# Moving the transposes and output products of the stick-breaking heads to later steps of the projection that covers them

## The chip, the cores and the metric

The kernel runs on one core of one Trainium2 chip. The metric is the device time of one execution in microseconds (us), as the median of the runs shown. Engines are named as in the profile: PE (TensorE matmuls), PEld (its weight loads), DVE (VectorE), ACT (ScalarE), POOL (GpSimd), SP (the queue that issues most DMAs).

## The reference, cut to what matters

A trunk of two layers over 256 positions of width 2048, all in float32. The first layer mixes sparse attention (10 heads, "A") with dilated attention (6 heads, "B"); the second mixes stick-breaking attention (8 heads, "C") with forgetting attention (8 heads, "D"). Each layer is one norm, one wide input projection, the heads, a gate, one output projection and the residual sum. The part that the change touches most is the stick-breaking head:

```python
z = jnp.einsum('bqhd,bshd->bhqs', qb, k).astype(F32) * (HEAD_DIM ** -0.5)
before = (key_pos[None, :] < qpos[:, None])[None, None]
log_1m = jnp.where(before, jax.nn.log_sigmoid(-z), 0.0)
tail = lax.cumsum(log_1m, axis=3, reverse=True) - log_1m
w = jnp.where(before, jnp.exp(jax.nn.log_sigmoid(z) + tail), 0.0)
return jnp.einsum('bhqs,bshd->bqhd', w.astype(v.dtype), v)
...
return x + (y * jax.nn.silu(gate)) @ w_out
```

## The kernel before, in words

The weights (about 165 MB) stream in once, cut into jobs. A job is the projection of both 128-row halves of the activations with one block of weight columns, mostly 512 wide: q, k, v and gate of one head of B, C or D, or q and gate of two heads of A. The jobs of the second layer are C0, F1, G1, C2 to C7, D0 to D7; F1 (264 wide: q and k of head C1, and the forget columns) and G1 (256 wide: its v and gate) share the columns of one head. A job walks over 16 row tiles of 128. To keep float32 accuracy on matmuls of a rounded type, each weight tile is split into an upper part (`whi`, by ACT, line 269) and the rest (`wlo`, by DVE, line 270), and each row tile takes three products for each half of the rows (lines 305, 306, 308). Splits cover two row tiles at a time (a "half" in the code; here a pair), so a job has eight pairs, and `split` (line 342) is called so that the split of a pair stands in the program three pairs ahead of its products.

Nothing reorders the work: the order is the order in which the code is written (manual schedule). What is left of a head after its job's projection (evacuating PSUM, transposes, scores, softmax or stick-breaking sums, products with v) is a generator that is started when its job's products have all been issued. It is advanced from inside the next jobs' projections: `tick` (line 293) counts a step for each row tile of a 512-wide job (for about each second row tile in F1 and G1), and a generator that said `yield n` goes on after n steps. So a 512-wide job offers 16 steps, and each engine gets the head's instructions between those of the running projection, in its own queue.

A stick-breaking head, in that order: at once, `scaled_qk` and `vg1` take q, k, v and gate out of PSUM (ACT lines 737, 749, 402; DVE lines 738, 751, the reciprocal 752, two products 755 that write the gate tile `u`, and 405). Then `stick` yields, and on PE `turn` (line 364) transposes q and k (four) and the gate `u` (two); ACT and DVE split the result (373, 374, 375) and ACT copies the gate (422, `uT`). After two steps come the scores (PE 800 and 379 to 381, then DVE `z` 803, ACT 805 to 807, DVE 808, the cut 392 and 393 into `sph` and `spl`), after five more the sums `pW` (812 to 815, then 816, 817, 820), one step on `pl` (822), and some steps on `weigh_out`: the products with v (379 to 381 and 430), the product with the gate (435, `y`) and its cut into `yh` and `yl` (392, 393).

`heads_a` does two sparse heads per job in the same manner; its last yields are the ones ahead of `turned(1, ...)`, the transposes of the second head's weights, and ahead of the products with v (687 to 689).

Of the kernel before, what the change touches and what calls it, by code (L numbers as in the profile page):

```python
# [159 lines left out]
def trunk(ctx, tc, x, xT, g1, w0, wo0, w1, wo1, bf, gf, consts, rope, out):  # L160
# [186 lines left out]
    def rotate(dst, src, cos, sin, r, m):  # L347

        n = r * m
        t1 = hp.tile([P, 512], F32, name="rot1", tag="rt1")  # L350
        t2 = hp.tile([P, 512], F32, name="rot2", tag="rt2")
        pair = lambda a: a.rearrange("p (r m two) -> p r m two", r=r, two=2)
        wide = lambda a: a.rearrange("p (r m) -> p r m", r=r)
        cb = cos.unsqueeze(1).to_broadcast([P, r, m]) if r > 1 else wide(cos)
        sb = sin.rearrange("p (m two) -> p m two", two=2).unsqueeze(1)
        sb = sb.to_broadcast([P, r, m // 2, 2]) if r > 1 else pair(sin)
        nc.vector.tensor_tensor(wide(t1[:, 0:n]), wide(src), cb, op=OP.mult)
        nc.vector.tensor_tensor(pair(t2[:, 0:n]), pair(src)[:, :, :, ::-1], sb, op=OP.mult)  # L358
        nc.gpsimd.tensor_tensor(dst, t1[:, 0:n], t2[:, 0:n], op=OP.add)  # L359

    def turn(srcs):
        pt = pa.tile([P, 512], F32, name="tp", tag="tp", bufs=2)
        for i, s in enumerate(srcs):
            nc.tensor.transpose(pt[:, i * P:(i + 1) * P], s, ident)  # L364
        return pt
# [24 lines left out]
    def cut(dst, src):  # L390

        nc.scalar.activation(dst[0], src, AF.Copy)  # L392
        nc.vector.tensor_tensor(dst[1], src, dst[0].bitcast(F32), op=OP.subtract)
# [18 lines left out]
    def gates(u, sc):  # L412

        for th in range(NT):
            t = slice(th * P, (th + 1) * P)
            nc.vector.tensor_scalar(u[:, t], u[:, t], sc[:, th:th + 1], None, op0=OP.mult)
# [23 lines left out]
    def soft(qk, nb):  # L440

        q0, k0, q1h, q1l, kh, kl = qk
        pS = pa.tile([P, 384], F32, name="s", tag="s", bufs=1)
        nc.tensor.matmul(pS[:, 0:P], q0, k0, start=True, stop=True)  # L444
        three(pS[:, P:384], q1h, q1l, kh, kl)
        sn = hp.tile([P, 384], F32, name="sn", tag="sn", bufs=2)
        nm = hp.tile([P, NT], F32, name="nm", tag="nm", bufs=2)
        l = hp.tile([P, NT], F32, name="l", tag="l", bufs=2)
        for th, s in BLK:
            nc.vector.tensor_tensor_reduce(sn[:, s], pS[:, s], nb[:, s], op0=OP.add, op1=OP.min, scale=1.0,  # L450
                                           scalar=3.0e38, accum_out=nm[:, th:th + 1])
            nc.scalar.activation(sn[:, s], sn[:, s], AF.Exp, scale=-1.0, bias=nm[:, th:th + 1],  # L452
                                 accum_out=l[:, th:th + 1])
        return sn, l

    def factor(l, rs):
        sc = hp.tile([P, NT], F32, name="sc", tag="sc", bufs=2)
        nc.vector.reciprocal(sc, l)
        if rs is not None:
            nc.vector.tensor_tensor(sc, sc, rs, op=OP.mult)  # L460
        return sc
# [178 lines left out]
    def heads_a(ps, h):  # L640
        qk = hp.tile([P, 512], F32, name="qk", tag="qk")
        u = hp.tile([P, 2, NT, P], F32, name="u2", tag="u2", bufs=1)
        tgs = {}
        for th in range(NT):
            rotate(qk[:, th * 256:(th + 1) * 256], ps[th][:, 0:256], rt[:, th, 0:P], rt[:, th, 256:384], 2, P)
            tgs[1 - th] = hp.tile([P, 256], F32, name="tg", tag="tg")
            nc.scalar.activation(tgs[1 - th], ps[1 - th][:, 256:512], AF.Tanh, scale=hr0[:, 1 - th:2 - th])
        for th in (1, 0):
            nc.vector.scalar_tensor_tensor(u[:, :, th, :], tgs[th].rearrange("p (a b) -> p a b", a=2), 1.0,
                                           ps[th][:, 256:512].rearrange("p (a b) -> p a b", a=2),  # L650
                                           op0=OP.add, op1=OP.mult)
        yield 4
        pt = turn([qk[:, 0:P], qk[:, P:256], qk[:, 256:384], qk[:, 384:512]])
        f = hp.tile([P, 256], F32, name="qqf", tag="qkf", bufs=1)
        hi = hp.tile([P, 256], F32R, name="qqh", tag="qkh", bufs=1)
        lo = hp.tile([P, 256], F32R, name="qql", tag="qkl", bufs=1)
        nc.scalar.activation(hi, pt[:, 256:512], AF.Copy)
        nc.scalar.activation(f, pt[:, 0:256], AF.Copy)
        nc.vector.tensor_tensor(lo, pt[:, 256:512], hi.bitcast(F32), op=OP.subtract)
        yield 2  # L660
        js = [slice(j * P, (j + 1) * P) for j in range(2)]

        ph, pl = (hp.tile([P, 2, SEQ], F32R, name="pA" + n, tag="i" + n, bufs=1) for n in "hl")
        p1h, p1l = (hp.tile([P, 2 * P], F32R, name="pB" + n, tag="v") for n in "hl")

        def turned(j, pr):
            pt = turn([pr[:, 0:P], pr[:, P:SEQ], pr[:, SEQ:384]])
            cut((ph[:, j, :], pl[:, j, :]), pt[:, 0:SEQ])
            cut((p1h[:, js[j]], p1l[:, js[j]]), pt[:, SEQ:384])

        sm = []
        for j in range(2):
            sm.append(soft((f[:, js[j]], kA, hi[:, js[j]], lo[:, js[j]], kAh, kAl), nbA))
            yield 2
            gates(u[:, j].rearrange("p a b -> p (a b)"), factor(sm[j][1], hr0))
        yield 1
        turned(0, sm[0][0])
        yield 2
        turned(1, sm[1][0])
        pt = turn([u[:, j, th] for j in range(2) for th in range(NT)])  # L680
        uT = hp.tile([P, 512], F32, name="uTA", tag="rl")
        nc.scalar.activation(uT, pt, AF.Copy)
        yield 3
        po = pa.tile([P, 512], F32, name="o", tag="o", bufs=1)
        vh, vl = vAs
        flat = lambda t: t.rearrange("p a b -> p (a b)")
        three_of(po, vh[:, 0], vl[:, 0], flat(ph), flat(pl), True, False)
        o1 = po.rearrange("p (a b c) -> p a b c", a=2, b=2)[:, :, 1, :]
        three_of(o1, vh[:, 1], vl[:, 1], p1h, p1l, False, True)
        y = hp.tile([P, 512], F32, name="yA", tag="rl")  # L690
        nc.vector.tensor_tensor(y, po, uT, op=OP.mult)
        kt = YPOS[f"A{h}"]
        cut([flat(t[:, kt:kt + 2, :]) for t in ys], y)
# [102 lines left out]
    def stick_head(qk, v, uT, kt):  # L796

        k1, q1, k0h, k0l, qh, ql = qk
        pZ = pa.tile([P, 384], F32, name="s", tag="s", bufs=1)
        nc.tensor.matmul(pZ[:, 0:P], k1, q1, start=True, stop=True)  # L800
        three(pZ[:, P:384], k0h, k0l, qh, ql)
        z = hp.tile([P, 384], F32, name="z", tag="sn")
        nc.vector.tensor_tensor(z, pZ, smask, op=OP.add)
        sp = hp.tile([P, 384], F32, name="sp", tag="sp", bufs=1)
        nc.scalar.activation(sp, z, AF.Abs)
        nc.scalar.activation(sp, sp, AF.Exp, scale=-1.0)
        nc.scalar.activation(sp, sp, AF.Ln, bias=1.0)
        nc.vector.scalar_tensor_tensor(sp, z, 0.0, sp, op0=OP.max, op1=OP.add)
        cut((sph[:, P:512], spl[:, P:512]), sp)
        yield 5  # L810
        pW = pa.tile([P, 384], F32, name="s", tag="s", bufs=1)
        nc.tensor.matmul(pW, tris[0], sph[:, P:512], start=True, stop=False)
        nc.tensor.matmul(pW, tris[0], spl[:, P:512], start=False, stop=False)
        nc.tensor.matmul(pW[:, 0:256], tris[1], sph[:, 0:256], start=False, stop=False)
        nc.tensor.matmul(pW[:, 0:256], tris[1], spl[:, 0:256], start=False, stop=True)
        nc.vector.tensor_tensor(z, pW, z, op=OP.add)
        nc.scalar.activation(z, z, AF.Exp)
        ph = hp.tile([P, SEQ], F32R, name="ph", tag="ph", bufs=1)
        pl = hp.tile([P, SEQ], F32R, name="pl", tag="pl", bufs=1)
        nc.scalar.activation(ph, z[:, P:384], AF.Copy)  # L820
        yield 1
        nc.vector.tensor_tensor(pl, z[:, P:384], ph.bitcast(F32), op=OP.subtract)
        yield 2
        weigh_out(ph, pl, z[:, 0:P], v, uT, kt, True)

    def stick(qk, v, u, kt):
        yield 2
        t = qk_turned([qk[:, 384:512], qk[:, 256:384], qk[:, 0:P], qk[:, P:256]])
        uT = gate_turned(u, True)
        yield 2  # L830
        yield from stick_head(qk_of(t), v, uT, kt)
# [150 lines left out]
```

## Time and profile before

| | us |
|---|---|
| median of 3 runs | 937.32 (937.15 to 938.77) |
| profiled execution | 937.25 |
| its span, first to last instruction | 935.5 |
| PE busy | 916.2 |
| DVE busy | 618.4 |
| ACT busy | 488.4 |

The span is what lies between the first and the last instruction; 1.75 us of the profiled execution lie around it. Busy time of an engine is the time in which one of its instructions ran; the rest of the span it either waited for another engine or had nothing to do. PE's matmuls overlap by a little, so the start of one to the start of the next is the time that it costs, and the duration in a row is longer than that (a 512-wide product: starts 0.23 us apart, rows of 0.39). A row ends in brackets with the idle time of its engine just before it, and with the instruction that ended that wait.

### The profile page before, as it was taken

The numbers are of one execution on the slowest core, as the hardware profiler recorded it, in microseconds if no ns is written. First come the engines' busy times: TensorE is split into PE (matmuls) and PEld (weight loads), VectorE is DVE, ScalarE is ACT, GpSimd is POOL, SyncE is SP. The second block draws the span as 40 slices with busy tenths as digits, with TensorE's granted clock in tenths as the row PEclk, the third lists the DMA queues.
The fourth block names the chain that finished last, engine by engine and source line by source line (L and its number), as shares of the span: only waits on it lengthen the run. The fifth ranks groups of instructions, "written<-read, shape, count | busy, mean of one in ns | idle before, by whom it ended". The sixth has DMA issues, their size and how long they took to land.

```text
span 935.5 us, 12005 instructions
## 1 busy us (share of the span) xinstructions
PE 916.2 (98%) x4489; PEld 767.3 (82%) x4489; DVE 618.4 (66%) x1053; ACT 488.4 (52%) x859; POOL 48.5 (5%) x68
## 2 busy tenths in 40 slices
PE   9999999999999999999999999999999999999996
PEld 6988888888888888888798777777888888888886
DVE  7667877766666665555566666666767666666563
ACT  7645545555455555555465555555555555555450
POOL 0021100000000000000000000000000000000110
PEclk9999999999999999999999999999999999999999
DMA  9954454544544454455275444445655555555542
GB/s 360 355 190 168 149 180 166 192 141 178 180 141 147 163 185 176 180 186 187 88 231 191 168 180 150 141 159 180 227 174 169 177 181 186 180 180 180 180 180 91
DMA packets 27323, 168.78 MB, mean 180 GB/s; under 512 B 3168, under 2 KB 3712, under 8 KB 9344
## 3 DMA queue, kind: packets, MB, share of 16 engines
q1 hardware_dynamic: 25920, 164.70, 49.7%
q0 software_dynamic: 768, 2.12, 0.8%
q10 hardware_dynamic: 576, 1.19, 0.3%
q8 instruction: 35, 0.57, 0.2%
q14 instruction: 24, 0.20, 0.1%
HBM read 165.89 MB, written 2.11 MB: 180 GB/s over the span
## 4 chain that ended last, share of the span: by engine, by line
PE 92%; DVE 4%; ACT 2%; issue 2%; DMA 0%; POOL 0%; SPq 0%; POOLq 0%; DVEq 0%; ACTq 0%
PE pj L305 28%; PE pj L306 28%; PE pj L308 28%; PE tp L364 3%; DVE e L752 1%; DVE wlo L270 1%; PE s L380 1%; PE s L444 1%; PE o L430 1%; ACT whi L269 1%; DMA w0yh<-in_w_in_dram 0%; PE s L379 0%; PE o L380 0%; PE s L381 0%; ACT e L749 0%
## 5 line engine op out<-in xcount | busy, mean ns | idle before, releaser
L270 DVE TENSOR_TENSOR wlo<-raw,whi 128x1024 fp32r<-128x1024 f32 (+3 forms) x300 | 357.7, 1203 | 174.1 <-ACT whi L269 172.5
L305 PE MATMUL pj<-whi,xh 128*128 128x512 f32 (+3 forms) x992 | 383.9, 389 | 0.6 <-ACT whi L269 0.6
L306 PE MATMUL pj<-whi,xl 128*128 128x512 f32 (+3 forms) x992 | 376.8, 381 | 0.0
L269 ACT ACTIVATE whi<-raw 128x1024 fp32r<-128x1024 f32 (+3 forms) x300 | 301.4, 1024 | 77.7 <-PE pj L306 71.6
L308 PE MATMUL pj<-wlo,xh 128*128 128x512 f32 (+3 forms) x992 | 297.1, 381 | 0.1
L308 PEld LDWEIGHTS pj<-wlo,xh 128*128 128x128 f32 x992 | 183.5, 188 | 37.0 <-DVE wlo L270 0.5
L305 PEld LDWEIGHTS pj<-whi,xh 128*128 128x128 f32 x992 | 186.6, 188 | 32.8 <-ACT whi L269 1.8
L306 PEld LDWEIGHTS pj<-whi,xl 128*128 128x128 f32 x992 | 186.7, 188 | 31.3 <-DVE xl L518 0.2
L305 PE MATMUL pj<-whi,yh 128*128 128x512 f32 (+1 forms) x248 | 96.0, 387 | 0.0
L306 PE MATMUL pj<-whi,yl 128*128 128x512 f32 (+1 forms) x248 | 94.9, 383 | 0.0
L308 PE MATMUL pj<-wlo,yh 128*128 128x512 f32 (+1 forms) x248 | 76.7, 383 | 0.0
L308 PEld LDWEIGHTS pj<-wlo,yh 128*128 128x128 f32 x248 | 46.6, 188 | 9.2
L305 PEld LDWEIGHTS pj<-whi,yh 128*128 128x128 f32 x248 | 46.6, 188 | 8.7
L306 PEld LDWEIGHTS pj<-whi,yl 128*128 128x128 f32 x248 | 46.7, 188 | 8.6
L452 ACT ACTIVATE sn<-sn,nm 128x128 f32<-128x128 f32 (+1 forms) x48 | 21.5, 449 | 55.3 <-DVE nm L450 55.3
L392 ACT ACTIVATE yh<-y 128x256 fp32r<-128x256 f32 x22 | 9.2, 418 | 41.4 <-DVE y L437 24.0
L480 ACT ACTIVATE sq<-xs 128x512 f32<-128x512 f32 x23 | 14.3, 622 | 29.4 <-DVE xs L703 26.8
L752 DVE RECIPROCAL e<-e 128x256 f32<-128x256 f32 x16 | 28.1, 1753 | 0.5
L359 POOL TENSOR_TENSOR qk<-rot,rot 128x256 f32<-128x256 f32 x22 | 15.8, 738 | 238.3 <-DVE rot L358 238.3
L737 ACT ACTIVATE qk<-pj,rr 128x128 f32<-128x128 f32 x32 | 10.0, 364 | 29.3 <-PE pj L308 29.3
L364 PE MATMUL tp<-cons,u 128*128 128x128 f32 x64 | 12.0, 282 | 9.4 <-DVE u L755 9.1
L738 DVE TENSOR_SCALAR qk<-pj,rstd 128x128 f32<-128x128 f32 x32 | 9.8, 347 | 16.4 <-ACT qk L737 16.4
(226 smaller groups left out, 753.5 us busy)
## 6 DMA issues: line engine op xcount, KB each, us to landing
raw<-in_w_in_dram SPq DMA_DIRECT2D x108, 1024.0 KB, 4.8
raw<-in_w_out_dram SPq DMA_DIRECT2D x32, 1024.0 KB, 4.8
raw<-in_w_in_dram SPq DMA_DIRECT2D x4, 672.0 KB, 9.9
raw<-in_w_in_dram SPq DMA_DIRECT2D x4, 528.0 KB, 3.5
w0yl<-in_w_in_dram SPq DMA_DIRECT2D x4, 512.0 KB, 6.9
xs<-in_x_dram SPq DMA_DIRECT2D x4, 512.0 KB, 11.3
raw<-in_w_in_dram SPq DMA_DIRECT2D x4, 512.0 KB, 4.0
xst<-in_xT_dram SPq DMA_DIRECT2D x5, 256.0 KB, 6.2
```

Of the source, the lines that this page charges most:

```text
L269: nc.scalar.activation(hi, rw, AF.Copy)
L270: nc.vector.tensor_tensor(lo, rw, hi.bitcast(F32), op=OP.subtract)
L305: nc.tensor.matmul(o, a, wh, start=(kt == 0), stop=False)
L306: nc.tensor.matmul(o, b, wh, start=False, stop=False)
L308: nc.tensor.matmul(o, a, wl, start=False, stop=(kt == KT - 1))
L359: nc.gpsimd.tensor_tensor(dst, t1[:, 0:n], t2[:, 0:n], op=OP.add)
L364: nc.tensor.transpose(pt[:, i * P:(i + 1) * P], s, ident)
L452: nc.scalar.activation(sn[:, s], sn[:, s], AF.Exp, scale=-1.0, bias=nm[:, th:th + 1], accum_out=l[:, th:th + 1])
L480: nc.scalar.activation(j, xs[:, th, c * 512:(c + 1) * 512], AF.Square, accum_out=ss[:, i, th, c:c + 1])
L737: nc.scalar.activation(qk[:, th * 256:th * 256 + P], ps[th][:, 0:P], AF.Copy, scale=rr[:, sgn, th:th + 1])
L738: nc.vector.tensor_scalar(qk[:, th * 256 + P:(th + 1) * 256], ps[th][:, P:256], r1[:, th:th + 1], None, op0=OP.mult)
L752: nc.vector.reciprocal(e, e)
```

## The change

Three numbers, no other edit. A stick-breaking head turns q, k and gate four steps after its job's end instead of two (`stick`, line 827). The products with v stand three steps after the split of the weights `pl`, instead of two (`stick_head`, line 823). Of two sparse heads, the second's transposes, and the gate's that follow them, stand three steps after the first's instead of two (`heads_a`, line 678). All later parts of these heads move with them: the scores and sums of a stick-breaking head by two steps, its outputs by three, the outputs of two sparse heads by one. No instruction is added or taken away.

```diff
         turned(0, sm[0][0])
-        yield 2
+        yield 3
         turned(1, sm[1][0])
...
         nc.vector.tensor_tensor(pl, z[:, P:384], ph.bitcast(F32), op=OP.subtract)
-        yield 2
+        yield 3
         weigh_out(ph, pl, z[:, 0:P], v, uT, kt, True)
...
     def stick(qk, v, u, kt):
-        yield 2
+        yield 4
         t = qk_turned([qk[:, 384:512], qk[:, 256:384], qk[:, 0:P], qk[:, P:256]])
```

On PE in job F1, where head C0 is turned, the order before is, from the third row tile's last products on (`pj` are the two PSUM tiles of the job, `tp` is where the transposes go):

```order
L308 MATMUL pj_4215<-wlo,xh 128x264
L308 MATMUL pj_4216<-wlo,xh 128x264
L364 MATMUL tp<-cons,qk 128x128 x4
L364 MATMUL tp<-cons,u 128x128 x2
L305 MATMUL pj_4215<-whi,xh 128x264
L306 MATMUL pj_4215<-whi,xl 128x264
L305 MATMUL pj_4216<-whi,xh 128x264
L306 MATMUL pj_4216<-whi,xl 128x264
L308 MATMUL pj_4215<-wlo,xh 128x264
```

The turn stands after three of the 16 row tiles, in the middle of the second pair. Of the changed kernel, the same place of the turn, with the end of one row tile ahead of it:

```order
L305 MATMUL pj_4215<-whi,xh 128x264
L306 MATMUL pj_4215<-whi,xl 128x264
L305 MATMUL pj_4216<-whi,xh 128x264
L306 MATMUL pj_4216<-whi,xl 128x264
L308 MATMUL pj_4215<-wlo,xh 128x264
L308 MATMUL pj_4216<-wlo,xh 128x264
L364 MATMUL tp<-cons,qk 128x128 x4
L364 MATMUL tp<-cons,u 128x128 x2
L305 MATMUL pj_4215<-whi,xh 128x264
```

It now stands after seven row tiles, in the middle of the fourth pair, so that pair's `wlo` is wanted ahead of the turn.

On DVE at the same place, from the end of job C0 on (`pj_4035` and `pj_4036` are C0's PSUM tiles, the 528-wide `wlo` are F1's pairs), before:

```order
L738 TENSOR_SCALAR qk<-pj_4036,rstd 128x128
L751 TENSOR_SCALAR e<-e 128x256
L752 RECIPROCAL e<-e 128x256
L755 SCALAR_TENSOR_TENSOR u<-pj_4035,rstd,e 128x128
L755 SCALAR_TENSOR_TENSOR u<-pj_4036,rstd,e 128x128
L405 SCALAR_TENSOR_TENSOR v<-pj_4035,rstd,v 128x128
L270 TENSOR_TENSOR wlo<-raw,whi 128x528 x2
L375 TENSOR_TENSOR qkl<-tp,qkh 128x384
L270 TENSOR_TENSOR wlo<-raw,whi 128x528 x2
L803 TENSOR_TENSOR z<-s,cons 128x384
```

And in the changed kernel:

```order
L752 RECIPROCAL e<-e 128x256
L755 SCALAR_TENSOR_TENSOR u<-pj_4035,rstd,e 128x128
L755 SCALAR_TENSOR_TENSOR u<-pj_4036,rstd,e 128x128
L405 SCALAR_TENSOR_TENSOR v<-pj_4035,rstd,v 128x128
L270 TENSOR_TENSOR wlo<-raw,whi 128x528 x4
L375 TENSOR_TENSOR qkl<-tp,qkh 128x384
L270 TENSOR_TENSOR wlo<-raw,whi 128x528
L270 TENSOR_TENSOR wlo<-raw,whi 128x512
L803 TENSOR_TENSOR z<-s,cons 128x384
```

Up to the first `wlo` nothing moved; two more `wlo` stand ahead of `qkl`.

On DVE at the end of job C2 (`y` and `yl` are the outputs of head C1, `pj_4576` and `pj_4577` the PSUM tiles of C2), before:

```order
L822 TENSOR_TENSOR pl<-z,ph 128x256
L270 TENSOR_TENSOR wlo<-raw,whi 128x1024
L435 TENSOR_TENSOR y<-o,uT 128x128 x2
L393 TENSOR_TENSOR yl<-y,yh 128x256
L270 TENSOR_TENSOR wlo<-raw,whi 128x1024 x2
L738 TENSOR_SCALAR qk<-pj_4576,rstd 128x128
L738 TENSOR_SCALAR qk<-pj_4577,rstd 128x128
```

And in the changed kernel:

```order
L822 TENSOR_TENSOR pl<-z,ph 128x256
L270 TENSOR_TENSOR wlo<-raw,whi 128x1024 x2
L435 TENSOR_TENSOR y<-o,uT 128x128 x2
L393 TENSOR_TENSOR yl<-y,yh 128x256
L738 TENSOR_SCALAR qk<-pj_4576,rstd 128x128
L738 TENSOR_SCALAR qk<-pj_4577,rstd 128x128
```

In the stretch shown, `y` and `yl` had two splits between them and the job's end; now they come right ahead of the first evacuation of the next head.

## Rows read from the trace of the kernel before

**Rows 1.** The page's busy times: engine, us, share of the span, instructions.

```profile
PE 916.2 (98%) x4489; PEld 767.3 (82%) x4489; DVE 618.4 (66%) x1053; ACT 488.4 (52%) x859; POOL 48.5 (5%) x68
```

**Rows 2.** Waits of PE: line <- releaser: us in total, times, longest us.

```profile
PE tp L364 <- DVE u L755: 9.1, 8, 1.8
PE s L892 <- DVE mhalf L888: 1.2, 1, 1.2
PE pj L305 <- ACT whi L269: 0.6, 2, 0.5
PE o L380 <- DVE pl L822: 0.6, 1, 0.6
PE tp L364 <- DVE u L416: 0.2, 1, 0.2
```

**Rows 3.** Windows: us, busy (instructions) by engine, then PEclk, DMA share, GB/s.

```profile
460.46:643.00 182.54, 174.00 (x916) 148.44 (x915) 122.06 (x181) 101.97 (x181) 2.01 (x3) 1.00 0.48 171
643.00:838.00 195.00, 193.86 (x922) 161.25 (x921) 132.28 (x222) 103.01 (x193) 5.43 (x8) 1.00 0.54 185
```

**Rows 4.** Timeline of PE in job C4, head C3: start us, us, instruction.

```profile
540.04 0.39 PE L305 MATMUL pj<-whi,xh 128*128 128x512 f32 x1
...
541.40 0.39 PE L305 MATMUL pj<-whi,xh 128*128 128x512 f32 x1
...
542.77 0.60 PE L364 MATMUL tp<-cons,qk 128*128 128x128 f32 x4
...
544.50 0.44 PE L364 MATMUL tp<-cons,u 128*128 128x128 f32 x2 [1.14 <-DVE u L755]
...
544.70 0.48 PE L305 MATMUL pj<-whi,xh 128*128 128x512 f32 x1
...
545.01 0.40 PE L306 MATMUL pj<-whi,xl 128*128 128x512 f32 x1
...
547.89 0.28 PE L380 MATMUL s<-qkl,qkh 128*128 128x256 f32 x1
```

**Rows 5.** Timeline of DVE in the same stretch.

```profile
543.84 0.61 DVE L755 SCALAR_TENSOR_TENSOR u<-pj,rstd,e 128x128 f32<-128x128 f32 x2
...
545.75 0.55 DVE L375 TENSOR_TENSOR qkl<-tp,qkh 128x384 fp32r<-128x384 f32 x1
```

**Rows 6.** Timeline of DVE and ACT, end of job C5, outputs of head C4.

```profile
586.10 0.49 DVE L435 TENSOR_TENSOR y<-o,uT 128x128 f32<-128x128 f32 x2 [0.55 <-PE o L430]
...
586.62 0.42 ACT L392 ACTIVATE yh<-y 128x256 fp32r<-128x256 f32 x1 [2.33 <-DVE y L435]
...
587.07 0.43 DVE L393 TENSOR_TENSOR yl<-y,yh 128x256 fp32r<-128x256 f32 x1 [0.49 <-ACT yh L392]
...
589.52 1.23 DVE L270 TENSOR_TENSOR wlo<-raw,whi 128x1024 fp32r<-128x1024 f32 x1 [0.27 <-ACT whi L269]
...
591.77 0.35 DVE L738 TENSOR_SCALAR qk<-pj,rstd 128x128 f32<-128x128 f32 x1 [1.02 <-ACT qk L737]
```

**Rows 7.** Timeline of PE and DVE in job F1, head C0.

```profile
460.46 0.28 PE L305 MATMUL pj<-whi,xh 128*128 128x264 f32 x1
...
461.19 0.28 PE L305 MATMUL pj<-whi,xh 128*128 128x264 f32 x1
...
465.02 0.41 PE L364 MATMUL tp<-cons,u 128*128 128x128 f32 x2 [1.78 <-DVE u L755]
...
465.04 1.32 DVE L270 TENSOR_TENSOR wlo<-raw,whi 128x528 fp32r<-128x528 f32 x2
```

**Rows 8.** Timeline of PE and DVE in job G1 and at the turn of its head.

```profile
475.30 0.28 PE L305 MATMUL pj<-whi,xh 128*128 128x256 f32 x1
...
475.77 0.61 DVE L738 TENSOR_SCALAR qk<-pj,rstd 128x128 f32<-128x128 f32 x2 [0.34 <-ACT qk L737]
...
477.95 0.69 DVE L270 TENSOR_TENSOR wlo<-raw,whi 128x512 fp32r<-128x512 f32 x1 [0.35 <-ACT whi L269]
...
493.18 0.44 PE L364 MATMUL tp<-cons,u 128*128 128x128 f32 x2 [0.50 <-DVE u L755]
```

## The prediction

> **What bounds the kernel now.** PE does. The page's first part has it busy for 916.2 of 935.5 us, DVE for 618.4, ACT for 488.4 [rows 1], so an edit is worth what it takes out of PE's idle time, and nothing else. I read the waits of PE next: apart from the start and the tail after the last product, nearly all of it is one line. The transposes of the gate waited eight times for the DVE instruction that writes the gate tile `u`, 9.1 us in all; one product with v waited once for `pl`, 0.6; the sparse and dilated heads gave one wait of 0.2 [rows 2]. The windows put the eight where the stick-breaking heads are: from F1's start to D0's, PE is idle for 8.5 of 182.5 us, and in the 195 us behind that, of which the first holds the last of the eight, for 1.1 [rows 3].
>
> The timeline of job C4 shows what one such wait is. The job starts at 540.04, a step takes 1.36 (541.40 less 540.04), and after two steps PE transposes q and k at once and then stands still for 1.14 us, until 544.50 [rows 4]. DVE takes q and k from PSUM, forms the gate's reciprocal and writes `u` from 543.84 to 544.45 [rows 5]. PE asked for `u` at 544.50 - 1.14 = 543.36, that is 3.32 us into the job, and it came after 4.41. PE keeps its order, so the weight products behind the transposes wait too, although their splits are there.
>
> **The change part by part.** *The turn, two steps later.* In a 512-wide job PE asks for `u` 2 x 1.36 = 2.73 us later, 6.05 us into the job. Of the eight waits six are 1.14, G1's head has 0.50 [rows 8], C0's 1.78 [rows 7]: 6 x 1.14 + 0.50 + 1.78 = 9.12. The longest is shorter than the two steps, so none is left if `u` is not written later. What can make it later is the next part.
>
> *The outputs, three steps later.* They took 586.10 to 587.50 on DVE and ACT (`y` 0.49, `yh` 0.42, `yl` 0.43), some four us before the next job's evacuation, with two splits in between [rows 6]. Now they stand right ahead of it. The job's last split waits for a buffer that PE frees at the same place as before and ends at 589.52 + 1.23 = 590.75; then `y`, `yh`, `yl` end near 592.15, where the next `qk` began at 591.77 [rows 6]. So the evacuation, and with it `u`, comes about 0.4 us late: 4.8 us into the job, where PE asks at 6.05. Cover 1.2 us; if it is gone, each us of delay costs six to seven us in all. Cost taken: nothing. The wait of 0.57 for `pl` has a step more and goes.
>
> *The scores.* They keep their two steps from the turn, but `qkl` has two splits ahead of it now instead of one. From the end of `u`: 0.25 for the rest of v, 1.2 and 1.2 for the two splits, 0.55 for `qkl` [rows 5], so it ends near 544.45 + 3.2 = 547.65, with the 0.4 from above at 548.05. PE wants it at 547.89 [rows 4], less the wait of 1.14, plus 2.73: 549.48. Cover 1.4 us, nothing charged. The sums, `pl` and the outputs keep or lengthen their distances.
>
> *F1, where a wait comes back.* F1's row tiles are narrow: 461.19 - 460.46 = 0.73 us each [rows 7], and splits stand only three pairs, six row tiles, ahead. The fourth pair's `wlo` is queued on DVE behind C0's evacuation and reciprocal: the two splits there run from 465.04 for 1.32, so the first ends at 465.74 [rows 7]. Today the wait of 1.78 for `u` hides that. Without it PE is through six row tiles at 460.46 + 6 x 0.727 = 464.82, and wants that `wlo` four products (0.49) later, at 465.31. It waits some 0.43, with the signal's way some 0.47. The turn stands behind this row tile now and finds `u` done. So C0's 1.78 gives 1.31.
>
> *G1 and the job behind it.* With all that F1 starts to end 1.31 us earlier, near 473.97. G1's fourth pair stands on DVE behind F1's evacuation, which began at 475.77; that split ends at 477.95 + 0.69 = 478.64 [rows 8]. PE wants it three pairs (4.3), the sums of C0 (0.6: 1280 columns at 0.23 for 512) and four products (0.5) after G1's start: at 479.35. So even a DVE that is not a bit earlier than today leaves 0.7 us. Likewise the gate of G1's head in job C2 has 2.73 us more where it lacked 0.50, but three splits of 1.2 and C0's outputs now crowd DVE at G1's end. From below nothing, from above the 0.5 that was there and 0.1 more: I take 0.1, near the lower end, since each single distance that I can work out has cover.
>
> *Sparse heads.* Their transposes and products waited for nothing but the one 0.2, which is a dilated head's [rows 2]; the step more costs and gives nothing. Their products with v now fall into the next job but one, behind its first row tile, and buffers of the next head's v wait for them. ACT does that evacuation at the start of a job whose first three pairs are split already, over 8 us of products (six steps of 1.36), and the step plus those six products (three of 512 columns at 0.23, three of 256 at half of it) take 2.4.
>
> *Sum,* on the profiled execution: 937.25 - 9.12 - 0.57 + 0.47 + 0.10 = **928.1 us**. That execution is 0.07 below the median, so it stands for the median too. No DMA, matmul or split is added.
>
> **Rivals.** *Handed on in the short jobs.* DVE is the crowded engine around F1 and G1; if its splits and outputs stop PE there wherever the wait for `u` did, only the six waits of 1.14 are won: 937.25 - 6.84 = 930.4. For it speaks that F1 already shows one such place, against it the 0.7 us at G1. Everything between 929 and 930.4 belongs to it.
>
> *More than the waits.* Behind the wait in job C4 the second product starts 0.31 us after the first (544.70, 545.01) [rows 4], where a step of six products in 1.36 has 0.23; if the 0.08 were the restart's price, eight times that go as well, and without the 0.1 the time is 927.4; without F1's wait too, 926.9. Against it: a slow start behind transposes need not be the wait's, and these rows don't tell the two apart.
>
> *The bubble is not for `u`.* First the row: the wait ends with DVE's write of `u` in all eight cases [rows 2], and it is 0.50 where no `qk` is taken out ahead of it and 1.78 in the narrow job [rows 7, 8], so it follows DVE's queue. In the kernel it could also be a shortage of the two PSUM tiles `tp`, which a later turn would not mend: the time would stay at 937.2. The Trainium skill (Perfetto Trace Analysis, section Identifying Performance Opportunities) says that a gap that repeats on the engine that should be saturated can mean that SBUF or PSUM is short for the next tile. By that rule nothing is won; the trace disagrees, since the first `tp` tile is filled without a wait and ACT, which empties them, is not named for this line.
>
> *Slower: the scores wait in place of the gate.* If DVE's queue of evacuation, outputs and two splits runs late as a whole, `qkl` is the last to come, and all work behind the scores waits, in the six wide jobs and G1's. It decides from 1.4 us beyond what I worked out, and loses more than is won from about 1.4 + 9.1 / 7 = 2.7 us on: at 3.2 us, 7 x (3.2 - 1.4) = 12.6 is lost and 9.2 won, 940.7. Against it: the whole of what was moved ahead of `qkl` is one split (1.2, in the sum already) and outputs of 1.4, of which 0.4 are in the sum.
>
> **How the numbers follow.** My forecast, 927.4 to 929: 0.73. Handed on in the short jobs: 0.14. More: 0.05. Not for `u`, or the change lost in some like way, within 0.2%: 0.05. Slower: 0.03. A difference of 0.2%, 1.9 us, is about what a measurement here can tell from no change. The first three are faster by more than that: 0.92; same 0.05; slower 0.03. The range takes in the second and third: 926.9, where neither wait comes back and the restarts are cheaper, to 930.6, the 930.4 with the runs' own scatter of 0.2.
>
> **What would show it.** Of the changed kernel: no wait of PE's line 364 for line 755; none of the second v product for `pl`; one new wait of a product of line 308 for `wlo` in F1, 0.3 to 0.6 us, about 5.3 us after F1's start; the jobs C3 to D0 shorter by 1.14 us each from start to start; the jobs from D1 on and all of the first layer as long as before; the granted clock at 1.00 as now [rows 3]. A wait of the scores for `qkl`, or of line 364 for `u` still, in the wide jobs would prove me wrong on DVE's cover; waits for splits in G1 would make the second case.

## The result, and the profile of the changed kernel

The changed kernel takes 925.18 us (median of 4 runs, 924.87 to 925.54) where the kernel before took 937.28 in the same comparison: a ratio of 0.9868, 95% interval 0.985 to 0.9885, 12.1 us less. The forecast was 928.1, a range of 926.9 to 930.6: the right direction and place, but a gain of 9.2 us where it is 12.1. One execution of the kernel with only the sparse heads' gate transposes later (below) took 1311.73 us at a granted clock of 0.65; the comparisons leave it out.

| | before | changed |
|---|---|---|
| profiled execution, us | 937.25 | 925.54 |
| span, us | 935.5 | 923.7 |
| PE busy, us | 916.2 | 913.3 |
| PE idle in the span, us | 19.3 | 10.4 |

The page's first part of the changed kernel (busy us, share of the span, instructions), which answers to [rows 1]:

```profile
PE 913.3 (99%) x4489; PEld 767.7 (83%) x4489; DVE 618.0 (67%) x1053; ACT 488.0 (53%) x859; POOL 48.5 (5%) x68
```

The same 4489 matmuls are now busy for 2.9 us less. PE's idle time fell by 8.9 us, near the 9.2 of the forecast; the rest of the gain came out of what the profile counted as work.

The waits of PE in the changed kernel (line <- releaser: us in total, times, longest), to be read against [rows 2]:

```profile
PE s L892 <- DVE mhalf L888: 1.2, 1, 1.2
PE pj L305 <- ACT whi L269: 1.2, 1, 1.2
PE pj L308 <- DVE wlo L270: 0.3, 1, 0.3
PE tp L364 <- DVE u L416: 0.2, 1, 0.2
```

The eight waits for `u` are gone, the one for `pl` too, and one new wait for a split has come: it is in F1, as the timeline of PE there shows (answers to [rows 7]):

```profile
465.07 0.51 PE L308 MATMUL pj<-wlo,xh 128*128 128x264 f32 x2 [0.34 <-DVE wlo L270]
465.41 0.60 PE L364 MATMUL tp<-cons,qk 128*128 128x128 f32 x4
465.85 0.38 PE L364 MATMUL tp<-cons,u 128*128 128x128 f32 x2
```

The wait of 1.2 for `whi` is in the first job, 7.75 us into the program (0.6 before). It was 0 to 0.8 in the profiles of the experiments below, 0.8 in a second profile of the changed kernel itself, so it scatters from one execution to the next, and nothing that the change moves stands there.

Windows by stretch (columns as in [rows 3]: length, busy us and instructions of PE, PEld, DVE, ACT and POOL, then PEclk, DMA share, GB/s) tell where the 11.8 us of span went. Three stretches of the kernel before: from F1's first product to D0's, job D0, and the sparse heads' jobs from A2's start to P0's:

```profile
460.46:642.72 182.26, 173.72 (x914) 148.20 (x913) 122.06 (x181) 101.69 (x180) 2.01 (x3) 1.00 0.48 170
642.72:668.38 25.66, 24.52 (x117) 20.35 (x116) 17.57 (x26) 14.10 (x25) 1.81 (x3) 1.00 0.59 211
192.25:345.63 153.38, 153.28 (x746) 127.36 (x745) 101.45 (x212) 79.27 (x152) 8.62 (x12) 1.00 0.47 165
```

The same stretches of the changed kernel:

```profile
459.74:632.19 172.45, 172.10 (x914) 148.31 (x913) 121.18 (x181) 100.55 (x180) 2.02 (x3) 1.00 0.52 182
632.19:656.49 24.30, 24.30 (x118) 20.38 (x117) 17.61 (x27) 13.98 (x25) 1.81 (x3) 1.00 0.57 197
192.53:344.91 152.38, 152.38 (x747) 127.46 (x746) 101.86 (x212) 80.40 (x152) 8.62 (x12) 1.00 0.47 167
```

The stick-breaking stretch is 9.81 + 1.36 = 11.17 us shorter (its idle time only by 8.19 + 1.14 = 9.33), and the sparse heads' jobs, where 0.1 us was idle, by 1.00. Together that is 12.17; the jobs ahead of A2, the first above all, give 0.28 back (A2 starts at 192.53 instead of 192.25), and the rest is as long as it was within some 0.1.

The turn in job C4 shows how a wait can cost more than its bracket. In the changed kernel (timeline of PE):

```profile
540.49 0.60 PE L364 MATMUL tp<-cons,qk 128*128 128x128 f32 x4
540.92 0.38 PE L364 MATMUL tp<-cons,u 128*128 128x128 f32 x2
541.06 0.47 PE L305 MATMUL pj<-whi,xh 128*128 128x512 f32 x1
541.37 0.39 PE L306 MATMUL pj<-whi,xl 128*128 128x512 f32 x1
```

From the first transpose to the first product behind is 0.57 us here, where it was 544.70 - 542.77 = 1.93 [rows 4]: 1.36 less, for a bracket of 1.14. A transpose's row is 0.27 long while the next one starts 0.11 after it, so 0.16 us of the wait lay under the row of the transpose ahead of it; and the second transpose of `u` came 0.165 behind the first instead of 0.11.

The sparse heads had such a wait that no bracket named at all. Before, PE and DVE in job A6:

```profile
263.66 0.49 PE L364 MATMUL tp<-cons,sn 128*128 128x128 f32 x3
264.17 0.63 PE L364 MATMUL tp<-cons,u 128*128 128x128 f32 x4
264.56 0.47 PE L305 MATMUL pj<-whi,xh 128*128 128x512 f32 x1
```

```profile
263.73 0.29 DVE L393 TENSOR_TENSOR pBl<-tp,pBh 128x128 fp32r<-128x128 f32 x1 [0.34 <-ACT pBh L392]
```

The changed kernel at the same place:

```profile
264.93 0.49 PE L364 MATMUL tp<-cons,sn 128*128 128x128 f32 x3
265.26 0.60 PE L364 MATMUL tp<-cons,u 128*128 128x128 f32 x4
265.62 0.47 PE L305 MATMUL pj<-whi,xh 128*128 128x512 f32 x1
```

Three transposes at 0.11 are 0.33 us, as after; before, the fourth came 0.51 behind the first. It writes a PSUM tile `tp`, of which there are two, and the older one was still being read by DVE's `pBl` of the first head, until 264.02.

### The profile page after: what moved, and what is told of

Read it like the earlier page. It is cut to its first block, busy times and chain, and to the rows that moved or that the text cites. A ratio compares the mean times of both kernels' runs of the same rounds, so it can differ in the third digit from the quotient of the medians.

```text
span 923.7 us, 12023 instructions
## 1 busy us (share of the span) xinstructions
PE 913.3 (99%) x4489; PEld 767.7 (83%) x4489; DVE 618.0 (67%) x1053; ACT 488.0 (53%) x859; POOL 48.5 (5%) x68
## 4 chain that ended last, share of the span: by engine, by line
PE 96%; DVE 1%; issue 1%; DMA 1%; ACT 1%; POOL 0%; SPq 0%; POOLq 0%; DVEq 0%; ACTq 0%
PE pj L305 29%; PE pj L306 29%; PE pj L308 29%; PE tp L364 3%; PE s L380 1%; DMA w0yh<-in_w_in_dram 1%; DVE wlo L270 1%; PE s L444 1%; PE o L430 1%; PE s L379 0%; PE s L381 0%; PE o L380 0%; PE o L379 0%; PE o L381 0%; PE tp L720 0%
## 5 line engine op out<-in xcount | busy, mean ns | idle before, releaser
L373 ACT ACTIVATE qkh<-tp 128x384 fp32r<-128x384 f32 x22 | 10.8, 491 | 26.2 <-PE tp L364 26.1
L392 ACT ACTIVATE ph<-tp 128x256 fp32r<-128x256 f32 x14 | 5.4, 382 | 27.9 <-PE tp L364 27.9
```

The lines of the kernel that those rows point to most:

```text
L373: nc.scalar.activation(hi, pt[:, P:512], AF.Copy)
```

## The experiments

Two theories of the 2.9 us were put up. Theory A: the forecast priced the waits by the idle time in the rows, and a wait costs its distance from start to start; and the sparse heads have a wait that no row names. Theory B: the waits cost what the rows show, and the outputs and the sparse heads, which were moved too, bring the rest in some other way. All runs are compared with the kernel before on the same chip (937.1 to 937.4).

### The three moves one by one

The turn alone:

```diff
     def stick(qk, v, u, kt):
-        yield 2
+        yield 4
```

> The kernel before with the turn of the stick-breaking heads alone moved from two steps to four. Two theories of the 12.1 us that the whole change brought. Theory A (a wait costs its start-to-start distance): the idle time in a row leaves out 0.16 us that the modelled duration of the transpose ahead of the wait covers, and the second transpose behind the wait starts 0.06 late, so the eight waits are worth 10.9 us and not the 9.1 that the rows show; F1's split gives back 0.5 to 0.6. It expects 10.3 us less than before, about 927.0, with the wait for pl in G1 still there in part. Theory B (a wait costs what its row shows; the other 2.9 us come from the outputs and the sparse heads, which were moved too): 9.1 less 0.4, about 928.6.

It took 926.26 us (ratio 0.9882, interval 0.9869 to 0.9895): 10.9 less. Theory A's 10.3 is near, theory B's 8.6 is not. Its waits of PE, besides the program's start, are one row:

```profile
PE pj L308 <- DVE wlo L270: 0.3, 1, 0.3
```

The wait for `pl` went too, with the sums and `pl` two steps further from G1's start, and G1 is 0.75 us shorter (13.29 instead of 14.04); that is the 0.7 between the expectation and the run.

The sparse heads alone:

```diff
         turned(0, sm[0][0])
-        yield 2
+        yield 3
         turned(1, sm[1][0])
```

> The kernel before with the second sparse head's transposes alone moved by one step. Theory A: the five jobs with sparse heads lose a delay of 0.2 us each that no row names (the first transpose of the gate starts 0.29 us behind the one ahead of it where 0.11 is usual): 1.0 us less, 936.2. By what the rows of waits show there is nothing to win: 937.2.

It took 936.23 us (ratio 0.9988, interval 0.9979 to 0.9997): 1.0 less, as theory A had it. With the turn alone that makes 11.9 of the 12.1.

Only the gate's transposes of the sparse heads one step later, everything else in place:

```diff
         turned(1, sm[1][0])
+        yield 1
         pt = turn([u[:, j, th] for j in range(2) for th in range(NT)])
...
-        yield 3
+        yield 2
```

> The kernel before, but of the two sparse heads only the gate's transposes stand one step later; the second head's transposes and the products with v stay where they were. If the hidden 0.2 us per job is a wait for the PSUM tile that the first head's transposes filled (two such tiles, the gate's is the third), one step is enough to free it and the same 1.0 us is won as with the whole move: 936.2. If it comes from where the second head's transposes or the products with v stand in the row of projections, nothing is won: 937.2.

It took 936.57 us (ratio 0.9995, interval 0.9985 to 1.0005, single executions from 936.14 to 939.77), which cannot be told from no change. The trace is clearer. Job A6 in the kernel before, in this one and in the changed one (windows: length, PE busy):

```profile
243.93:269.79 25.86, 25.84 (x128) 21.47 (x127) 17.30 (x37) 13.40 (x26) 1.44 (x2) 1.00 0.45 163
```

```profile
243.33:269.05 25.72, 25.72 (x129) 21.44 (x127) 17.30 (x37) 13.39 (x26) 1.44 (x2) 1.00 0.46 163
```

```profile
242.79:268.45 25.66, 25.66 (x128) 21.48 (x126) 17.39 (x38) 13.63 (x26) 1.44 (x2) 1.00 0.45 164
```

0.14 of the 0.20 us go by moving nothing but the transposes that reuse the tile, and 0.14 to 0.17 in the other four jobs with sparse heads. So most of the hidden delay is a wait for that tile and not the place of the other transposes or of the products with v; what the 0.06 that stay are is not shown.

### The eight waits taken away without a move

```diff
         nc.vector.tensor_scalar(e, e, 1.0, 3.0e38, op0=OP.add, op1=OP.min)
-        nc.vector.reciprocal(e, e)
```

> The kernel before with nothing moved, but the reciprocal of the gate left out (line 752, 1.75 us on DVE in all heads of the second layer), so that the gate is computed without it and written 1.8 us earlier. All eight waits should be gone without moving anything. Theory A (start-to-start): 10.9 us less, and F1's split comes 1.8 us earlier too, so that nothing is given back: 926.4, or 925.6 if the wait for pl goes as well. Theory B (idle of the rows): 928.2, or 927.6. A time near 937 would say that the waits were not for DVE's write of u.

This kernel leaves the reciprocal of the gate out, so it computes other values, and only its time is of use. It took 925.3 us (ratio 0.9872, interval 0.9855 to 0.9888): 11.9 less, 1.1 beyond theory A and 2.9 beyond theory B. Its waits of PE still name `pl`, and no `u` of line 755:

```profile
PE o L380 <- DVE pl L821: 0.6, 1, 0.6
PE pj L305 <- ACT whi L269: 0.5, 1, 0.5
PE tp L364 <- DVE u L416: 0.2, 1, 0.2
```

The turn of job C4's head stands at the old place and costs what it costs in the changed kernel, 0.57 us:

```profile
539.13 0.60 PE L364 MATMUL tp<-cons,qk 128*128 128x128 f32 x4
539.56 0.38 PE L364 MATMUL tp<-cons,u 128*128 128x128 f32 x2
539.70 0.47 PE L305 MATMUL pj<-whi,xh 128*128 128x512 f32 x1
```

So the extra 0.22 us of each wait belongs to the wait and not to the move. What lies beyond theory A is in the forgetting heads' jobs, where this edit works too: D2 to D7 take 24.04 us each here and 24.20 in the kernel before, though no row of either names a wait there. The kernel with the later forgetting scores, below, reaches the same 24.04 by another way.

### One step instead of two

```diff
     def stick(qk, v, u, kt):
-        yield 4
+        yield 3
```

> The changed kernel with the turn at three steps instead of four. A step is 1.36 us and the largest of the wide jobs' waits was 1.14, so theory A expects no wait in the jobs C3 to D0, with 0.1 us of cover; in F1 a wait of 0.3 for u in place of the 0.34 for the split; in C2, where the gate is written 5.5 us into the job and wanted after 4.5, up to 1.0. So 925.0 to 926.3 us. The rival, that outputs and splits ahead of the evacuation need the whole second step, expects waits of 0.4 or more in each of the wide jobs: 928 or more.

It took 926.4 us (ratio 0.9885, interval 0.987 to 0.9899): 1.2 more than with four steps, just beyond what theory A gave, and far from the 928 of the rival. PE waits for `u` twice, in F1 and in C2:

```profile
463.90 0.41 PE L364 MATMUL tp<-cons,u 128*128 128x128 f32 x2 [0.33 <-DVE u L755]
...
491.03 0.44 PE L364 MATMUL tp<-cons,u 128*128 128x128 f32 x2 [0.38 <-DVE u L755]
```

In F1 the second step gains nothing: the job takes 13.37 us here and 13.43 with four steps, where it waits for its split instead. In C2 it is worth 0.60 (24.93 and 24.33), and in each of the six wide jobs 0.12 (24.41 and 24.29). There `u` ends 0.05 us ahead of its transposes, which come 0.16 behind the last of q and k instead of 0.11, and no bracket shows that.

### A better version

The changed kernel was run again beside three that build on it.

> The changed kernel as it is, on the chip of the runs that build on it. 925.2 us.

It took 925.35 us (ratio 0.9871).

The forgetting heads, whose turn nobody had touched:

```diff
         t = qk_turned([qk[:, 0:P], qk[:, P:256], qk[:, 384:512], qk[:, 256:384]])
-        yield 2
+        yield 3
         yield from softmax_head(qk_of(t), biases[h], v, u, None, HC + h)
```

> The changed kernel, with the scores of the forgetting heads three steps behind their turn instead of two. No row names a wait there, but in the eight heads the second score product starts 0.05 and the third 0.10 us later than in the other heads, just behind the write of qkl. If such delays that no row names are waits (theory A), 8 x 0.15 = 1.2 us go: 924.0. If only what a row names is a wait: 925.2.

It took 924.02 us (ratio 0.9856): 1.3 less than the changed kernel, as theory A had it. From D1's first product to Q1's, windows of the changed kernel and of this one:

```profile
656.49:850.21 193.72, 193.72 (x921) 161.11 (x920) 130.77 (x224) 101.47 (x192) 3.61 (x5) 1.00 0.53 181
```

```profile
656.84:849.19 192.35, 192.35 (x921) 160.54 (x920) 130.16 (x224) 103.53 (x192) 3.62 (x5) 1.00 0.55 183
```

Both have PE busy for all of it, with the same 921 instructions, and one is 1.37 us shorter: waits of some 0.17 us in each of eight heads that hide whole under the modelled ends. The profiled execution lost 0.6 of that again in job C2, for which see the outputs alone, below.

F1's wait for its split:

```diff
         elif k == "C":
+            if h == 0:
+                split(st["split"] + 1)
             start(head_c(ps, h))
```

> The changed kernel, with the split of F1's fourth pair put ahead of the evacuation of head C0 on ACT and DVE. It should take away the wait of 0.34 us (0.5 to 0.6 start to start) for that split in F1; C0's gate is then written some 0.7 us later, 5.1 us into F1, and wanted at 5.5. 924.6 us; 925.2 or more if that cover is not there.

It took 924.49 us (ratio 0.9861), 0.86 less than the changed kernel. The step of the forecast that charged F1 a returning wait was right: it can be taken out by the order of two engines' work.

> The changed kernel with both of these: the forgetting heads' scores a step later and F1's fourth split ahead of C0's evacuation. If the two are independent, 1.2 + 0.6 less than the changed kernel: 923.4.

Both together took 923.06 us (ratio 0.9846, interval 0.9831 to 0.9861): 2.3 less than the changed kernel, the sum of the two within 0.1, and the best kernel here. F1 in the changed kernel and in this one:

```profile
459.74:473.17 13.43, 13.09 (x108) 12.88 (x107) 8.96 (x16) 8.27 (x20) 0.00 (x0) 1.00 0.38 118
```

```profile
459.25:472.06 12.81, 12.81 (x108) 12.81 (x107) 8.90 (x17) 8.12 (x20) 0.00 (x0) 1.00 0.43 124
```

### The outputs alone, which make it slower

```diff
-        yield 2
+        yield 3
         weigh_out(ph, pl, z[:, 0:P], v, uT, kt, True)
```

> The kernel before with the outputs of the stick-breaking heads alone moved from two to three steps behind the splits. Theory A: only the one wait for pl goes, 0.7 to 0.8 us start to start: 936.5; the eight waits of line 364 stay at 1.1 each. Theory B: the outputs carry part of the 2.9 us, one to two us more than that: 934.5 to 935.5.

Both theories missed: 940.1 us (ratio 1.0024, interval 1.0013 to 1.0035), with single executions from 936.17 to 941.56. The fastest are where theory A had them. What the profiled execution (940.6 us) loses is in one place, job C2, which takes 29.43 us instead of 25.04. PE there, and ACT ahead of it:

```profile
491.00 0.60 PE L364 MATMUL tp<-cons,qk 128*128 128x128 f32 x4
494.89 0.44 PE L364 MATMUL tp<-cons,u 128*128 128x128 f32 x2 [3.29 <-DVE u L755]
```

```profile
489.81 1.06 ACT L269 ACTIVATE whi<-raw 128x1024 fp32r<-128x1024 f32 x1 [3.46 <-DMA raw<-in_w_in_dram]
490.78 0.35 ACT L749 ACTIVATE e<-pj,nr 128x128 f32<-128x128 f32 x1
```

ACT waits for weights of C2's third pair, which PE will not need for some microseconds, and the evacuation of G1's gate, which PE needs next, is queued behind that split. So `u` is late by the lateness of a load.

Why was the load late? With the outputs further back, G1's last split ends earlier, and with it the next load's request comes earlier: at 483.28, 1.2 us behind the one ahead of it, instead of 485.02, 2.7 us behind, in the kernel before. The one ahead is the load that ACT waited for. An attempt to hold that request back by one split:

```diff
+            if st.pop("held", None):
+                load()
             if (i + 1 == len(halves) or halves[i + 1][1] != pi) and (pi >= len(FIRST) - 1 or kt + m == 10):
-                load()
+                if jobs[ji][2] == "G1" and kt + m == KT:
+                    st["held"] = True
+                else:
+                    load()
```

> The kernel with the outputs alone moved, which came out 2.9 us slower than before, with one weight load issued later: the piece that is requested when G1's last pair is split is requested one split later, behind the first pair of C2. Theory: in that kernel the outputs no longer stand between G1's last splits, so the load is issued 1.2 us behind the one ahead of it instead of 2.7, the two share the transfer, the one ahead lands after 7.6 us instead of 5.0, ACT waits for it with the next head's evacuation queued behind, and PE waits 3.3 us for the gate in job C2. With the load held back that wait falls to the 0.50 of before, and the time to 936.4, with a spread below 1 us. Rival: the landing is late for another reason (the evacuation itself, or transfers of other queues): 939 to 941 again.

> The kernel with the outputs alone moved, once more, on the chip of the run with the held load: 940 us, single executions from 936 to 941.6.

The held one took 937.03 us (936.03 to 940.21; ratio 1.0004, interval 0.9996 to 1.0013), the repeat 938.09 (936.69 to 940.44; ratio 1.0015, interval 1.0005 to 1.0025). But the edit did not do what it was to do. In its trace the request stands at 483.09, as early as ever:

```profile
483.09 0.33 SPq L243 DMA_DIRECT2D raw<-in_w_in_dram  x1
```

In the profile the waits of the queue SP end nearly all with a split by DVE (`wlo`, 107 waits, 584 us), that is with the buffer that the load is to fill; the place in the program, one split later, was not what this request waited for. So this run says nothing on the theory of the request, except by chance: its profiled execution took 936.12 us. With the request at the same early time the load ahead landed after 4.9 us, just when PE freed the buffer of the split; ACT waited 0.72 us, which the profile puts down to PE, and PE for `u` only 0.55:

```profile
486.89 1.06 ACT L269 ACTIVATE whi<-raw 128x1024 fp32r<-128x1024 f32 x1 [0.72 <-PE pj L313]
```

In the profile of the repeat (938.35 us) the wait ahead of that split was 2.79, for the weights, and the wait for `u` 2.62:

```profile
489.05 1.06 ACT L269 ACTIVATE whi<-raw 128x1024 fp32r<-128x1024 f32 x1 [2.79 <-DMA raw<-in_w_in_dram]
```

Three profiles with these requests at the same place thus have PE's wait in C2 follow ACT's wait ahead of that split (3.46 and 3.29, 2.79 and 2.62, 0.72 and 0.55: each time 0.17 less), with the load under way for 7.6, 7.0 and 4.9 us. That chain is shown. What makes the load land late in one execution and not in the next stays open, and the early request alone is not enough for it.

The same chain reaches the kernels with the turn at four steps. There too two loads of C2 are requested 1.2 us apart, and the second lands after 7.3 us in the changed kernel and after 8.5 in the profile of the kernel with the later forgetting scores, where ACT and then PE wait:

```profile
487.52 1.06 ACT L269 ACTIVATE whi<-raw 128x1024 fp32r<-128x1024 f32 x1 [0.44 <-DMA raw<-in_w_in_dram]
...
492.60 0.44 PE L364 MATMUL tp<-cons,u 128*128 128x128 f32 x2 [0.38 <-DVE u L755]
```

Job C2 takes 24.93 us there instead of 24.33.

## Why the forecast was wrong, point by point

The step that failed is that an edit is worth "what it takes out of PE's idle time, and nothing else". Idle time fell by 8.9 us, near the forecast; the time fell by 12.1. Of the miss some 2 us lie in the price of the waits and 1 us in the sparse heads.

*What bounds the kernel, and the place of the eight waits:* right. All eight are gone, and without moving anything a faster `u` takes them away as well. The rival that the bubble was a shortage of PSUM tiles fell for them. It holds for the sparse heads: there the same 0.2 us stood in each of five jobs, and a `tp` tile was the cause of most of it. The Trainium skill (Perfetto Trace Analysis, section Identifying Performance Opportunities) says that a gap that repeats on the engine that should be saturated can mean too little PSUM for the next tile. For the sparse heads this trace agrees, with 0.2 us in each of five jobs, though no row shows these as a gap.

*The price of the eight waits, 9.12:* this is the term of the sum that was mis-sized. In the six wide jobs a wait cost 1.36 to 1.38 us and not 1.14: the window from F1 to D0 and D0 itself are 11.17 shorter, where the forecast's terms for that stretch (9.12 + 0.57 - 0.47 - 0.10) make 9.12. The idle time in brackets counts from the modelled end of the transpose ahead, which lies 0.16 us behind the time at which the next one starts where nothing waits; with the 0.06 by which the second transpose of `u` comes late that is 0.22 for each wait. The forecast had this number in its own front: a product's row is 0.39 long and the next starts 0.23 later. It then took 543.36 = 544.50 - 1.14 for the time at which PE asked for `u`; four transposes at 0.11 behind 542.77 would have given 543.21. Its own rival "more than the waits" blamed the restart and had 0.05. The Trainium skill (Perfetto Trace Analysis, section Identifying the Most-Contended Engine) says that the busy share of matmuls is not a good measure of how close a kernel is to its roofline, because they are pipelined. For the narrower point, that PE's busy time is not a fixed amount of work, this trace has a number: the same 4489 instructions are busy for 916.2 us and for 913.3.

*The wait for `pl`, 0.57:* right in kind, but too small in the same way: with the outputs alone moved, job G1 is 0.84 us shorter (13.20 instead of 14.04).

*Sparse heads, nothing:* wrong, 1.0 us. The forecast looked for waits in the rows of waits alone.

*F1, where a wait comes back:* right. 0.47 was forecast; it is 0.34 in the bracket and 0.6 by the length of F1 without it (13.43 and 12.81).

*G1 and C2, 0.10:* no wait there in the changed kernel's profile, though the place is the one with least cover: `u` ends 5.62 us into C2 and its transposes stand at 5.91. A wait of 0.38 shows in C2 with the turn at three steps, and another of 0.38 in the kernel with the later forgetting scores, behind a late load.

*The outputs, cost nothing:* right within the whole change, and the working for the wide jobs too. DVE in job C4 of the changed kernel:

```profile
538.81 0.61 DVE L755 SCALAR_TENSOR_TENSOR u<-pj,rstd,e 128x128 f32<-128x128 f32 x2
...
541.92 0.56 DVE L375 TENSOR_TENSOR qkl<-tp,qkh 128x384 fp32r<-128x384 f32 x1
```

`u` ends 4.40 us into the job (it started at 535.02), not even the 0.4 later that was charged, and `qkl` at 7.46, well ahead of the score product that reads it, at 9.21. But alone the same move came out 2.9 and 1.0 us slower in two comparisons, by a chain that the forecast did not have: split ahead of its need, its load late, evacuation queued behind. Two more steps at the turn cover it in the profiles of the changed kernel, though not in every execution, as the wait of 0.38 in C2 shows. So the rival on the other side had a place (a crowded DVE) and a price, and the real danger was on ACT, one job wide.

## What to carry to other kernels

Price a wait by the distance from start to start of the two instructions around it, less the distance that the same pair has where nothing waits: the idle time in a row is too small by what the modelled row of a pipelined instruction covers, and short waits do not appear at all. To find these, compare the same pair of instructions across heads and jobs. A step that has cover for its own producer may still wait when that producer's queue stands behind a load, so a load's scatter (here 4.9 to 7.6 us for the same load of the same kernel) belongs into the cover.

## What the runs showed of the hardware that was not expected

Behind a turn the second product starts 0.31 us after the first, in the changed kernel as before (541.06 and then 541.37), where 0.23 is usual, whether or not PE waited. So the rival's 0.08 belongs to every turn and not to a wait. Nor is it a price. The last of the six transposes starts at 541.03, five times 0.11 behind 540.49, and the first product only 0.03 later, where transposes are 0.11 apart; 0.11 and 0.23 behind 541.03 give the 541.37 at which the second product starts. The first product's row is early by what the second's is late.

After the wait of 3.29 us in job C2 of the kernel with the outputs alone moved, TensorE's granted clock fell to the lower of its two levels. Two windows there (PEclk, the third value from the end, is the granted clock in parts of the full 2.4 GHz), during the wait and from 0.8 us behind it:

```profile
491.50:494.90 3.40, 0.11 (x2) 0.01 (x1) 3.26 (x6) 2.00 (x5) 1.33 (x2) 1.00 0.14 53
495.70:498.70 3.00, 3.00 (x8) 2.30 (x7) 2.22 (x3) 0.99 (x2) 0.00 (x0) 0.50 0.76 183
```

The twelve products of the two row tiles between the turn and the head's first `s`, cut, on PE's timeline of the same kernel:

```profile
495.09 0.48 PE L305 MATMUL pj<-whi,xh 128*128 128x512 f32 x1
...
497.45 0.63 PE L305 MATMUL pj<-whi,xh 128*128 128x512 f32 x1
497.87 0.63 PE L306 MATMUL pj<-whi,xl 128*128 128x512 f32 x1
...
499.51 0.38 PE L800 MATMUL s<-qkf 128*128 128x128 f32 x2
```

They start 0.42 us apart at the lower level (1.2 GHz), and all twelve take 4.42 us. In the kernel before the same stretch, behind a wait of 0.50, goes from 493.38 to 496.21, which is 2.83. Behind the wait of 2.62 in the repeat the clock stayed at 1.00. So the longer of the two waits cost 1.59 us more than its own length.
